# Expert weights of a mixture-of-experts layer: pieces of half the rows by all columns instead of all rows by half the columns

## Chip, cores and metric

One NeuronCore of a Trainium2 chip runs the whole program. The metric is the device time of one execution in microseconds (us). The kernel before took 2630.31 us, the median of three runs (2628.85 to 2637.18).

## The reference, cut to what matters

2048 tokens of width 1024 go through one layer: modulation, grouped attention beside a short convolution, an output projection, and then a mixture of 32 experts (4 groups, top 1; then top 2 of 8 experts). Everything is fp32. The part that the change touches is the norm ahead of the router and the experts:

```python
hx2 = rms_norm(x_new, norm2_g) * (1.0 + sc2) + sh2
...
def expert_block(args):
    xb, e = args
    return (jax.nn.silu(xb @ w_gate[e]) * (xb @ w_up[e])) @ w_down[e]
```

`w_gate` and `w_up` are 1024 x 768 per expert, `w_down` is 768 x 1024. Each expert's output row is scaled by the router's weight, summed over the token's two experts, gated and added to the stream; a last RMSNorm follows.

## The kernel before

**Stages.** Projections, attention and convolution take roughly the first 1440 us. In the stage called out_prep and the functions proj, norm2, logits and route (lines 704 to 950) each of 16 tiles of 128 tokens gets its output projection, the second norm (norm2, lines 816 to 820, result h2 stored to DRAM as h2d) and its routing. From about 1560 us on the 32 experts run, one after the other, in an order (PLAN, line 43) that mixes experts with many and with few tokens. The list CAPS (line 40) holds the padded token count C of each; 20 of them are above 128 (called wide here), 12 are 128 or below (narrow).

**Weights as a stream.** An expert's weights are six pieces of 1.5 MB (piece_src, line 1134). A piece of gate or up is all 1024 rows by 384 of the 768 columns, and a piece of down all 768 rows by 512 of the 1024 columns. Row k*128 + p lands in partition p, so a partition receives 8 runs of 1536 bytes for gate and up, and 6 runs of 2048 bytes for down. The DMA writes fp32 into a ring of five raw tiles (NRAW, line 46), issued by SP in line 1169. Stream.step (line 1173) then takes a third of a raw piece: ACT writes the fp16 high half (line 1192), and DVE subtracts it to make the fp16 low half (line 1194). Three steps finish a piece in a ring of six ready tiles wr. A raw tile is loaded again when its third step is done; a ready tile is written again when its piece is given back (done, line 1209).

**An expert.** Three matmuls (three, lines 1337 to 1340: high by high, high by low, low by high) stand for one fp32 product. gate_up (line 1342) goes over two column halves; for each of three column blocks f of a half it runs 24 matmuls into PSUM tile pg with the gate piece, then 24 into pu with the up piece. ACT makes silu of pg (sg, line 1356), DVE multiplies by pu (line 1357), ACT casts the product to the high half of a (line 1358), DVE makes the low half (line 1359). Three conversion steps follow each f but the last. For a wide expert, down (line 1369) then makes eight blocks of 128 columns in pairs: for both of a pair f = 0 to 4 first, 30 matmuls, and f = 5 behind them. For a narrow expert, down_rows (line 1387) streams 512 columns against the 128 or fewer tokens. Beside the gate and up groups, an iterator (beside, line 1514) transposes the previous expert's outputs and the next expert's gathered rows.

**What sets the order.** The program is written in the order above, and a scheduler places each engine's instructions; each engine then runs its own list strictly in order, so an instruction that waits holds back all behind it. The last two experts' pieces are interleaved in the same raw ring with six loads of acc for the final norm (final_item, line 1451).

Of the kernel before, what the change touches and what calls it, by code (L numbers as in the profile page):

```python
# [9 lines left out]
F32 = mybir.dt.float32  # L10
# [4 lines left out]
AF = mybir.ActivationFunctionType  # L15
OP = mybir.AluOpType
# [3 lines left out]
P = 128  # L20
D = 1024
S = 2048
CTX = 256
KT = D // P
# [8 lines left out]
DE = 768  # L33
FT = DE // P
# [24 lines left out]
def tile_block(ctx: ExitStack, tc: tile.TileContext, x, c, ctxt, c_ctx, w_mod, b_mod, norm1_g, w_in,  # L59
# [370 lines left out]
    if True:  # L430
# [267 lines left out]
        def mod_bc(i):  # L698
            return bass.AP(tensor=modrow.tensor, offset=modrow.offset + i * D, ap=[[0, P], [1, D]])
# [4 lines left out]
        def out_prep():  # L704
# [14 lines left out]
            nc.sync.dma_start(g2, bc(norm2_g, 0, D))  # L719
            B2 = dm["B2"] = dp.tile([P, D], F32, name="B2")  # L720
            nc.sync.dma_start(B2, mod_bc(SH2))

# [7 lines left out]
            yield  # L730
            V.scalar_tensor_tensor(A2, A2, 1.0, g2, op0=OP.add, op1=OP.mult)
            V.scalar_tensor_tensor(mc[:, 1], mc[:, 1], 1.0, mc[:, 2], op0=OP.add, op1=OP.mult)
            yield
# [3 lines left out]
            cB = dm["cB"] = dp.tile([P, NG + NE], F32, name="cB")  # L737
            V.tensor_copy(cB, pl[:, 0:NG + NE])
            yield
            for k in range(KT):  # L740
# [33 lines left out]
        def proj(bp, mf, mh, ml, xt, tt, banks, eng):  # L774
# [355 lines left out]
    wr_pool = [w1] * NEARLY  # L1130
    HE = DE // 2
    PW = KT * HE

    def piece_src(e, i):
        if i < 4:
            src = (w_gate, w_up)[i % 2][0, bass.ds(e, 1)].rearrange("a (k p) n -> p (a k) n", p=P)
            return src[:, :, (i // 2) * HE:(i // 2 + 1) * HE], KT
        src = w_down[0, bass.ds(e, 1)].rearrange("a (k p) n -> p (a k) n", p=P)
        return src[:, :, (i - 4) * 512:(i - 3) * 512], FT

    class Stream:
# [62 lines left out]
        def get(self, q):  # L1204
            while self.piece <= q:
                assert self.step()
            return self.ready[q].rearrange("p a (k n) -> p a k n", k=KT if q % 6 < 4 else FT)

# [91 lines left out]
    with ExitStack() as st:  # L1300
# [16 lines left out]
        def gather(il):  # L1317
            xg = []
            for i, (t, o, n) in enumerate(il):
                g_ = xp.tile([P, D], F32, name=f"xg{i}", bufs=3 - i)  # L1320
                G.indirect_dma_start(out=g_[:n, :], out_offset=None, in_=h2d[:, :],
                                     in_offset=bass.IndirectOffsetOnAxis(ap=t[:n, 0:1], axis=0))
                xg.append(g_)
            return xg

        def transposes(il, xg, xs):
            for (t, o, n), g_ in zip(il, xg):
                for b in range(2):
# [6 lines left out]
                    yield  # L1335

        def three(p_, w, k, cs, x, C, first, last):
            T.matmul(p_[:, :C], w[:, 0, k, cs], x[:, 0, k, :C], start=first, stop=False)  # L1338
            T.matmul(p_[:, :C], w[:, 0, k, cs], x[:, 1, k, :C], start=False, stop=False)  # L1339
            T.matmul(p_[:, :C], w[:, 1, k, cs], x[:, 0, k, :C], start=False, stop=last)  # L1340

        def gate_up(x, ws, q0, C, side=iter(())):
            a = xp.tile([P, 2, FT, CM], F16, name="a")
            for hf in range(2):
                gw, uw = ws.get(q0 + 2 * hf), ws.get(q0 + 2 * hf + 1)
                for f3 in range(3):
                    f = hf * 3 + f3
                    ps = []
                    for w, tag in ((gw, "pg"), (uw, "pu")):
                        p_ = pp.tile([P, 512], F32, name=tag)  # L1350
                        for k in range(KT):
                            three(p_, w, k, slice(f3 * P, (f3 + 1) * P), x, C, k == 0, k == KT - 1)
                        ps.append(p_)
                        next(side, None)
                    sg = sp.tile([P, CM], F32, name="sg")
                    A.activation(sg[:, :C], ps[0][:, :C], AF.Silu, scale=1.0 / WS)  # L1356
                    V.scalar_tensor_tensor(sg[:, :C], ps[1][:, :C], 1.0 / WS, sg[:, :C], op0=OP.mult, op1=OP.mult)  # L1357
                    A.copy(a[:, 0, f, :C], sg[:, :C])
                    V.tensor_sub(a[:, 1, f, :C], sg[:, :C], a[:, 0, f, :C])
                    for _ in range(3 if f < FT - 1 else 0):  # L1360
                        ws.step()
                ws.done(q0 + 2 * hf)
                ws.done(q0 + 2 * hf + 1)
            for w in side:
                if w == "wait":
                    break
            return a

        def down(a, ws, q0, C):
            yT = xp.tile([P, KT, CM], F32, name="yT")  # L1370
            for b in range(2):
                w = ws.get(q0 + 4 + b)
                for d2 in range(0, 4, 2):
                    py = [pp.tile([P, 512], F32, name=tag) for tag in ("pg", "pu")]
                    for fs in (range(FT - 1), (FT - 1,)):
                        for i in range(2):
                            for f in fs:
                                three(py[i], w, f, slice((d2 + i) * P, (d2 + i + 1) * P), a, C, f == 0, f == FT - 1)
                    for i in range(2):
                        d = b * 4 + d2 + i  # L1380
                        A.activation(yT[:, d, :C], py[i][:, :C], AF.Copy, scale=gt2c[:, d:d + 1])
                    ws.step()
                ws.done(q0 + 4 + b)
            return yT


        def down_rows(il, a, ws, q0):
            (t, o, n), = il
            y = sp.tile([P, D], F32, name="y", bufs=3)
            ws_ = [ws.get(q0 + 4 + b) for b in range(2)]  # L1390
            py = [pp.tile([P, 512], F32, name=tag) for tag in ("pg", "pu")]
            for fs in (range(FT - 1), (FT - 1,)):
                for b in range(2):
                    for f in fs:
                        for i, j in ((0, 0), (0, 1), (1, 0)):
                            T.matmul(py[b][:n, :], a[:, i, f, :n], ws_[b][:, j, f, :],
                                     start=(f == 0 and i + j == 0), stop=(f == FT - 1 and i == 1))
            for b in range(2):
                V.scalar_tensor_tensor(y[:n, b * 512:(b + 1) * 512], py[b][:n, :], t[:n, 1:2].bitcast(F32),
                                       gt2r[:n, b * 512:(b + 1) * 512], op0=OP.mult, op1=OP.mult)  # L1400
                ws.step()
                ws.step()
                ws.done(q0 + 4 + b)
            return t, n, y
# [202 lines left out]
```

## Time and profile before

| | us |
|---|---|
| median of 3 runs | 2630.31 |
| lowest and highest run | 2628.85, 2637.18 |
| the profiled execution | 2625.82 |
| its span, first to last instruction | 2624.0 |
| PE busy over the span | 2333.0 |
| DVE busy | 2064.2 |
| ACT busy | 1678.6 |

The profiled execution is 4.5 us below the median, and 1.8 us of it lie outside the span. Matmuls overlap each other in the profile (each is shown with its full latency, while one starts every 50 to 90 ns), so that short gaps of PE are covered by the record of the matmul before; the shares are read by stage, and waits from the list of waits.

### The profile page before, as it was taken

To read this page: it belongs to the slowest core of one execution; us is meant where nothing else is said; L and a number is where in the kernel's file an instruction comes from. 1 tells how busy PE (TensorE), PEld (TensorE's weight loads), DVE (VectorE), ACT (ScalarE), POOL (GpSimd) and SP (SyncE) were. 2 spreads that over 40 slices of the span, in tenths; PEclk is the share of its full clock that TensorE was granted. 3 is DMA by queue.
4 is the path that set the end of the run, shared out by engine and by line. 5 is a ranking of instruction groups with operands and counts; after the bars stand their busy time and mean duration, and the time that the engine had idled before them with its cause. 6 is when DMAs were issued, how large, how long until landed. Compare 5 with 4: busy or idle time off the path is not lost. (4 is left out here: it accounts for less than half of the span.)

```text
span 2624.0 us, 65043 instructions
## 1 busy us (share of the span) xinstructions
PE 2333.0 (89%) x26923; PEld 1791.5 (68%) x26923; DVE 2064.2 (79%) x3558; ACT 1678.6 (64%) x3170; POOL 726.3 (28%) x449
## 2 busy tenths in 40 slices
PE   7878898898999999888889949999999999999974
PEld 2545565665777755555555539998899988999953
DVE  4786789999777788878897657788788887788866
ACT  4554365566666676556656427777677777888854
POOL 2554114322222234435444331111111111211122
PEclk9888999999999999889998969999999999999987
DMA  7422423323111143212211569999999999999996
GB/s 279 145 90 88 127 78 115 125 82 108 50 52 34 34 93 81 64 52 80 58 64 52 191 197 336 338 326 304 307 355 350 349 334 344 340 335 340 358 311 247
DMA packets 320331, 499.27 MB, mean 190 GB/s; under 512 B 50466, under 2 KB 229022, under 8 KB 316959
## 3 DMA queue, kind: packets, MB, share of 16 engines
q1 hardware_dynamic: 281142, 429.41, 48.7%
q0 software_dynamic: 16032, 39.85, 6.0%
q10 hardware_dynamic: 22856, 25.82, 2.9%
q8 instruction: 212, 3.47, 0.5%
q14 instruction: 89, 0.72, 0.1%
HBM read 427.20 MB, written 67.90 MB: 189 GB/s over the span
## 5 line engine op out<-in xcount | busy, mean ns | idle before, releaser
L1194 DVE SCALAR_TENSOR_TENSOR wr<-raw,wr 128x1024 f16<-128x1024 f32 x576 | 685.4, 1218 | 118.8 <-ACT wr L1192 111.3
L1192 ACT ACTIVATE wr<-raw 128x1024 f16<-128x1024 f32 x576 | 580.4, 1054 | 57.3 <-DMA raw<-in_w_up_dram 22.9
L489 ACT ACTIVATE pf<-st 128x512 f32<-128x512 f32 x576 | 345.0, 599 | 284.2 <-PE st L488 226.9
L496 POOL TENSOR_TENSOR pl<-pf,ph 128x1024 f16<-128x1024 f32 x125 | 273.5, 2188 | 620.0 <-PE o L514 259.3
L461 DVE TENSOR_REDUCE mx<-mxp 128x1 f32<-128x512 f32 (+1 forms) x640 | 391.9, 628 | 65.1 <-PE mxp L460 63.6
L1339 PEld LDWEIGHTS <-wr 128*128 128x128 f16 x4032 | 397.4, 99 | 27.6 <-issue 24.6
L1340 PEld LDWEIGHTS <-wr 128*128 128x128 f16 x4032 | 397.2, 99 | 14.4 <-issue 9.9
L1338 PEld LDWEIGHTS <-wr 128*128 128x128 f16 x4032 | 397.1, 99 | 14.1 <-issue 11.3
L490 ACT ACTIVATE ph<-st 128x512 f16<-128x512 f32 x576 | 344.6, 598 | 0.0
L1338 PE MATMUL pg<-x,wr 128*128 128x152 f16 (+19 forms) x1536 | 293.9, 226 | 6.7 <-ACT sg L1356 3.8
L1338 PE MATMUL pu<-x,wr 128*128 128x152 f16 (+19 forms) x1536 | 293.7, 226 | 5.2 <-DVE sg L1357 5.1
L1340 PE MATMUL pu<-x,wr 128*128 128x152 f16 (+19 forms) x1536 | 293.1, 226 | 1.6 <-DVE wr L1194 0.8
L1340 PE MATMUL pg<-x,wr 128*128 128x152 f16 (+19 forms) x1536 | 293.5, 226 | 1.1 <-DVE wr L1194 1.0
L1339 PE MATMUL pg<-x,wr 128*128 128x152 f16 (+19 forms) x1536 | 293.8, 226 | 0.0
L1339 PE MATMUL pu<-x,wr 128*128 128x152 f16 (+19 forms) x1536 | 293.5, 226 | 0.0
L613 PE MATMUL z<-h,cwh 128*128 128x256 f16 x1536 | 275.1, 275 | 12.9 <-DVE vb L621 8.9
L460 PE MATMUL mxp<-k1T,q 128*128 128x512 f16 (+1 forms) x640 | 230.9, 364 | 41.5 <-DVE mx L461 40.5
L514 PE MATMUL o<-vh,pl 128*128 128x65 f16 x2304 | 246.2, 196 | 7.0 <-DVE pl L498 4.6
L512 PE MATMUL o<-vh,ph 128*128 128x65 f16 x2304 | 247.0, 197 | 0.3 <-ACT ob L521 0.2
L513 PE MATMUL o<-vlo,ph 128*128 128x64 f16 x2304 | 246.8, 195 | 0.0
L512 PEld LDWEIGHTS <-ph 128*128 128x128 f16 x2304 | 217.6, 99 | 25.2 <-issue 9.8
L487 PE MATMUL st<-q,k1T 128*128 128x512 f16 x576 | 222.5, 387 | 12.4 <-ACT ph L490 11.9
(349 smaller groups left out, 5541.6 us busy)
## 6 DMA issues: line engine op xcount, KB each, us to landing
raw<-in_w_down_dram SPq DMA_DIRECT2D x64, 1536.0 KB
raw<-in_w_gate_dram SPq DMA_DIRECT2D x63, 1536.0 KB
raw<-in_w_up_dram SPq DMA_DIRECT2D x63, 1536.0 KB
xt<-in_x_dram SPq DMA_DIRECT2D x32, 512.0 KB
h<-hs SPq DMA_DIRECT2D x16, 1024.0 KB
wmod<-in_w_mod_dram SPq DMA_DIRECT2D x64, 256.0 KB
w<-in_w_mod_dram SPq DMA_DIRECT2D x16, 512.0 KB
hs<-h ACTq DMA_DIRECT2D x8, 1024.0 KB
```

Source lines behind the costliest of these rows:

```text
L461: V.tensor_reduce(rowmax[u][:, j, i:i + 1], p_[:, :n], axis=AX.X, op=OP.max)
L489: A.activation(pf[:, i], p_, AF.Exp)
L490: A.activation(ph[:, i], p_, AF.Exp)
L496: G.tensor_tensor(pl, pf, ph, op=OP.subtract)
L512: T.matmul(po[:, j], ph[:, i, js], vh1[:, k, g], start=f, stop=False, skip_group_check=True)
L513: T.matmul(po[:, j, 0:HD], ph[:, i, js], vlo[:, k, g], start=False, stop=False, skip_group_check=True)
L613: T.matmul(z, w_[:, k, cs], h[:, a_, k, :], start=(n == 0), stop=(n == 3 * KT - 1))
L1192: A.activation(w[:, 0, sl], t[:, sl], AF.Copy, scale=WS)
L1194: V.scalar_tensor_tensor(w[:, 1, sl], t[:, sl], WS, w[:, 0, sl], op0=OP.mult, op1=OP.subtract)
L1338: T.matmul(p_[:, :C], w[:, 0, k, cs], x[:, 0, k, :C], start=first, stop=False)
L1339: T.matmul(p_[:, :C], w[:, 0, k, cs], x[:, 1, k, :C], start=False, stop=False)
L1340: T.matmul(p_[:, :C], w[:, 1, k, cs], x[:, 0, k, :C], start=False, stop=last)
```

## The change

A piece is now half the rows by all columns. The six pieces of an expert are gate, gate, up, up, down, down. For gate and up the rows are dealt so that partition p holds rows 8p to 8p+7; four of them by 768 columns lie one behind the other in DRAM, one run of 12288 bytes for each partition. A piece of down is three runs of 3072 bytes for each partition. The piece sizes, the rings, the conversions and the matmuls are the same in number and in shape.

Because row 8p + k now belongs to contraction step k, the normed tokens have to be dealt likewise: norm2 writes column 8q + k of the norm to place 128k + q (the multiply reads x and A2 with a step of 8 elements), and the shift B2 is copied once into the dealt order.

With a product needing both pieces of a matrix, gate_up runs its six gate groups first and its six up groups behind them. The silu of all six blocks is kept in one sg tile. One conversion step follows every group, and six follow in down, where both pieces are held to the end. The gathered rows have two buffers for each of their two tiles instead of three and two.

```diff
-    HE = DE // 2
-    PW = KT * HE
+    KN = (KT // 2, KT // 2, FT // 2)
+    PW = KT // 2 * DE
 
     def piece_src(e, i):
+        kn = KN[i // 2]
+        w_ = (w_gate, w_up, w_down)[i // 2][0, bass.ds(e, 1)]
         if i < 4:
-            src = (w_gate, w_up)[i % 2][0, bass.ds(e, 1)].rearrange("a (k p) n -> p (a k) n", p=P)
-            return src[:, :, (i // 2) * HE:(i // 2 + 1) * HE], KT
-        src = w_down[0, bass.ds(e, 1)].rearrange("a (k p) n -> p (a k) n", p=P)
-        return src[:, :, (i - 4) * 512:(i - 3) * 512], FT
+            src = w_.rearrange("a (p k) n -> p (a k) n", p=P)
+        else:
+            src = w_.rearrange("a (k p) n -> p (a k) n", p=P)
+        return src[:, (i % 2) * kn:(i % 2 + 1) * kn, :], kn
...
+        def dealt(t):
+            return t.rearrange("p (q k) -> p k q", k=KT)
+
         def norm2(bp, xt, r, eng):
             h2 = bp.tile([P, D], F32, name="h2")
-            V.scalar_tensor_tensor(h2, xt, r, dm["A2"], op0=OP.mult, op1=OP.mult)
+            V.scalar_tensor_tensor(h2.rearrange("p (k q) -> p k q", k=KT), dealt(xt), r, dealt(dm["A2"]), op0=OP.mult, op1=OP.mult)
...
+            B2 = dm["B2"] = dp.tile([P, D], F32, name="B2")
+            V.tensor_copy(B2.rearrange("p (k q) -> p k q", k=KT), dealt(b2))
...
-                g_ = xp.tile([P, D], F32, name=f"xg{i}", bufs=3 - i)
+                g_ = xp.tile([P, D], F32, name=f"xg{i}", bufs=2)
...
         def gate_up(x, ws, q0, C, side=iter(())):
             a = xp.tile([P, 2, FT, CM], F16, name="a")
-            for hf in range(2):
-                gw, uw = ws.get(q0 + 2 * hf), ws.get(q0 + 2 * hf + 1)
-                for f3 in range(3):
-                    f = hf * 3 + f3
...
+            sg = sp.tile([P, FT, CM], F32, name="sg", bufs=1)
+            for m in range(2):
+                w = ws.both(q0 + 2 * m)
+                for f in range(FT):
+                    p_ = pp.tile([P, 512], F32, name=("pg", "pu")[f % 2])
+                    for k in range(KT):
+                        three(p_, w, k, slice(f * P, (f + 1) * P), x, C, k == 0, k == KT - 1)
+                    next(side, None)
+                    if m == 0:
+                        A.activation(sg[:, f, :C], p_[:, :C], AF.Silu, scale=1.0 / WS)
+                    else:
+                        V.scalar_tensor_tensor(sg[:, f, :C], p_[:, :C], 1.0 / WS, sg[:, f, :C], op0=OP.mult, op1=OP.mult)
+                        A.copy(a[:, 0, f, :C], sg[:, f, :C])
+                        V.tensor_sub(a[:, 1, f, :C], sg[:, f, :C], a[:, 0, f, :C])
+                    ws.step()
+                ws.done(q0 + 2 * m)
+                ws.done(q0 + 2 * m + 1)
...
         def down(a, ws, q0, C):
             yT = xp.tile([P, KT, CM], F32, name="yT")
-            for b in range(2):
-                w = ws.get(q0 + 4 + b)
-                for d2 in range(0, 4, 2):
...
+            w = ws.both(q0 + 4)
+            for d in range(0, KT, 2):
...
+                for _ in range(1 + d // 2 % 2):
                     ws.step()
-                ws.done(q0 + 4 + b)
+            ws.done(q0 + 4)
+            ws.done(q0 + 5)
             return yT
```

The loads on SP's queue, around one expert of the middle of the stage (raw is a raw tile; the numbers behind the names are partitions by elements), before:

```order
L1169 DMA raw<-in_w_down_dram 128x6x512
L1169 ISA
L1169 DMA raw<-in_w_down_dram 128x6x512
L1169 ISA
L1169 DMA raw<-in_w_gate_dram 128x8x384
L1169 ISA
L1169 DMA raw<-in_w_up_dram 128x8x384
```

and with the change:

```order
L1178 DMA raw<-in_w_down_dram 128x3x1024
L1178 ISA
L1178 DMA raw<-in_w_gate_dram 128x3072
L1178 ISA
L1178 DMA raw<-in_w_gate_dram 128x3072
L1178 ISA
L1178 DMA raw<-in_w_up_dram 128x3072
```

The number of loads and their place among the others stay; a load of gate or up is one run of 3072 elements for each partition instead of eight of 384.

ACT at the end of gate_up of the wide expert with C = 148, where down begins (a is the product's high half, yT the output of down), before:

```order
L1356 ACTIVATE sg<-pg 128x148
L1358 CAST a<-sg 128x148
L1356 ACTIVATE sg<-pg 128x148
L1192 ACTIVATE wr<-raw 128x1024 x3
L1358 CAST a<-sg 128x148
L1192 ACTIVATE wr<-raw 128x1024 x2
L1381 ACTIVATE yT<-pg,gt2c 128x148
```

and with the change:

```order
L1201 ACTIVATE wr<-raw 128x1024
L1371 CAST a<-sg 128x148 x4
L1201 ACTIVATE wr<-raw 128x1024 x2
L1371 CAST a<-sg 128x148
L1201 ACTIVATE wr<-raw 128x1024 x2
L1391 ACTIVATE yT<-pg,gt2c 128x148
```

The cast of the last block, f = 5, stood behind three conversions and now stands behind two, and the four casts before it stand together.

DVE in the up groups of the same expert, with the change (sg is the product, wr the low half of a conversion):

```order
L1370 SCALAR_TENSOR_TENSOR sg<-pu,sg 128x148
L1203 SCALAR_TENSOR_TENSOR wr<-raw,wr 128x1024
L1372 TENSOR_TENSOR a<-sg,a 128x148
L1370 SCALAR_TENSOR_TENSOR sg<-pg,sg 128x148
L1372 TENSOR_TENSOR a<-sg,a 128x148
L1370 SCALAR_TENSOR_TENSOR sg<-pu,sg 128x148
L1203 SCALAR_TENSOR_TENSOR wr<-raw,wr 128x1024
L1372 TENSOR_TENSOR a<-sg,a 128x148
L1203 SCALAR_TENSOR_TENSOR wr<-raw,wr 128x1024 x11
```

The multiplications and subtractions of all six blocks stand in one phase with five conversions between them, and eleven conversions in a row follow.

## Rows read from the trace of the kernel before

**Rows 1.** The page: span, mean busy share of the DMA engines, GB/s, 40 slices.

```profile
span 2624.0 us, 65043 instructions
...
DMA  7422423323111143212211569999999999999996
GB/s 279 145 90 88 127 78 115 125 82 108 50 52 34 34 93 81 64 52 80 58 64 52 191 197 336 338 326 304 307 355 350 349 334 344 340 335 340 358 311 247
```

**Rows 2.** Windows: us, then busy PE, PEld, DVE, ACT, POOL; clock, DMA share, GB/s.

```profile
1600.00:1790.00 190.00, 189.22 (x2434) 178.02 (x2432) 151.19 (x200) 144.59 (x240) 35.13 (x19) 1.00 1.02 329
1790.00:2200.00 410.00, 387.21 (x5138) 361.50 (x5137) 335.14 (x445) 302.62 (x502) 64.16 (x40) 0.99 1.01 336
2200.00:2490.00 290.00, 281.30 (x4300) 274.27 (x4298) 233.26 (x312) 238.89 (x428) 48.07 (x34) 0.99 1.03 344
2490.00:2624.00 134.00, 77.78 (x980) 60.29 (x977) 86.44 (x126) 68.06 (x120) 30.99 (x31) 0.82 0.79 281
```

**Rows 3.** Waits from 1790 to 2200 us: total, times, longest.

```profile
ACT wr L1192 <- DMA raw<-in_w_up_dram: 19.5, 10, 4.8
ACT wr L1192 <- DMA raw<-in_w_down_dram: 16.5, 12, 4.1
...
PE pg L1338 <- ACT a L1358: 13.0, 8, 3.5
...
ACT wr L1192 <- DMA raw<-in_w_gate_dram: 6.7, 3, 3.4
...
PE pg L1339 <- DVE a L1359: 3.6, 7, 0.5
```

**Rows 4.** Waits from 2200 to 2490 us.

```profile
PE pg L1338 <- ACT a L1358: 5.7, 9, 1.1
...
PE pg L1339 <- DVE a L1359: 2.1, 8, 0.5
...
ACT wr L1192 <- DMA raw<-in_w_up_dram: 0.9, 1, 0.9
```

**Rows 5.** Timeline of ACT at 2195 us: start, duration, idle before and its releaser.

```profile
2195.36 2.95 ACT L1192 ACTIVATE wr<-raw 128x1024 f16<-128x1024 f32 x3 [3.39 <-DMA raw<-in_w_gate_dram]
```

**Rows 6.** Timeline of PE around the same place.

```profile
2193.78 0.23 PE L1339 MATMUL pg<-a,wr 128*128 128x152 f16 x1
...
2194.84 0.23 PE L1340 MATMUL pu<-a,wr 128*128 128x152 f16 x1
2198.57 0.23 PE L1338 MATMUL pg<-a,wr 128*128 128x152 f16 x1 [3.51 <-ACT a L1358]
```

**Rows 7.** DMA queues from 1700 to 2200 us: packets, MB, share of 16 engines.

```profile
q1 hardware_dynamic: 91076, 146.10, 84.8%
q0 software_dynamic: 8544, 19.21, 16.0%
```

**Rows 8.** DMA queue from 30 to 39 us, x, w_mod and w_in loads.

```profile
q1 hardware_dynamic: 1085, 3.67, 102.0%
```

**Rows 9.** DMA issues from 2490 to 2600 us: expert weights.

```profile
raw<-in_w_down_dram SPq DMA_DIRECT2D x4, 1536.0 KB
raw<-in_w_up_dram SPq DMA_DIRECT2D x3, 1536.0 KB
raw<-in_w_gate_dram SPq DMA_DIRECT2D x2, 1536.0 KB
```

**Rows 10.** Instructions from 2200 to 2490 us: count, busy us, mean ns.

```profile
L1192 ACT ACTIVATE wr<-raw 128x1024 f16<-128x1024 f32 x169 | 171.5, 1056 | 0.9 <-DMA raw<-in_w_up_dram 0.9
...
L1358 ACT CAST a<-sg 128x148 f16<-128x148 f32 x6 | 1.9, 310 | 6.3 <-DVE sg L1357 6.3
...
L1194 DVE SCALAR_TENSOR_TENSOR wr<-raw,wr 128x1024 f16<-128x1024 f32 x170 | 201.4, 1219 | 28.6 <-ACT wr L1192 24.3 <-issue 3.2
...
L1357 DVE SCALAR_TENSOR_TENSOR sg<-pu,sg 128x148 f32<-128x148 f32 x6 | 1.8, 304 | 2.5 <-PE ty L1412 2.5
```

**Rows 11.** Line 818: ns min/median/max.

```profile
L818 DVE SCALAR_TENSOR_TENSOR h<-xt,n2r,A x16: 1264/1285/3155, 1012.7 to 1529.8; 128x1024 f32<-128x1024 f32 x16
```

More of the change, by code (lines that the diff above doesn't have):

```diff
@@ L731, in out_prep @@
             V.scalar_tensor_tensor(A2, A2, 1.0, g2, op0=OP.add, op1=OP.mult)
+            b2 = dp.tile([P, D], F32, name="h2")
+            nc.sync.dma_start(b2, mod_bc(SH2))
             V.scalar_tensor_tensor(mc[:, 1], mc[:, 1], 1.0, mc[:, 2], op0=OP.add, op1=OP.mult)
@@ L1206, in get, with both @@
                 assert self.step()
-            return self.ready[q].rearrange("p a (k n) -> p a k n", k=KT if q % 6 < 4 else FT)
+            return self.ready[q].rearrange("p a (k n) -> p a k n", k=KN[q % 6 // 2])
+        def both(self, q):
+            return self.get(q), self.get(q + 1)
         def done(self, q):
@@ L1337, in three @@
         def three(p_, w, k, cs, x, C, first, last):
-            T.matmul(p_[:, :C], w[:, 0, k, cs], x[:, 0, k, :C], start=first, stop=False)
-            T.matmul(p_[:, :C], w[:, 0, k, cs], x[:, 1, k, :C], start=False, stop=False)
-            T.matmul(p_[:, :C], w[:, 1, k, cs], x[:, 0, k, :C], start=False, stop=last)
+            n = w[0].shape[2]
+            w_, kk = w[k // n], k % n
+            T.matmul(p_[:, :C], w_[:, 0, kk, cs], x[:, 0, k, :C], start=first, stop=False)
+            T.matmul(p_[:, :C], w_[:, 0, kk, cs], x[:, 1, k, :C], start=False, stop=False)
@@ L1342, in gate_up @@
+            T.matmul(p_[:, :C], w_[:, 1, kk, cs], x[:, 0, k, :C], start=False, stop=last)
         def gate_up(x, ws, q0, C, side=iter(())):
             a = xp.tile([P, 2, FT, CM], F16, name="a")
-            for hf in range(2):
-                gw, uw = ws.get(q0 + 2 * hf), ws.get(q0 + 2 * hf + 1)
-                for f3 in range(3):
-                    f = hf * 3 + f3
[L1348 to L1363, printed above, removed]
@@ L1370, in down @@
             yT = xp.tile([P, KT, CM], F32, name="yT")
-            for b in range(2):
-                w = ws.get(q0 + 4 + b)
-                for d2 in range(0, 4, 2):
[L1374 to L1378, printed above, removed]
-                    for i in range(2):
-                        d = b * 4 + d2 + i
-                        A.activation(yT[:, d, :C], py[i][:, :C], AF.Copy, scale=gt2c[:, d:d + 1])
+            w = ws.both(q0 + 4)
+            for d in range(0, KT, 2):
+                py = [pp.tile([P, 512], F32, name=tag) for tag in ("pg", "pu")]
+                for fs in (range(FT - 1), (FT - 1,)):
+                    for i in range(2):
+                        for f in fs:
+                            three(py[i], w, f, slice((d + i) * P, (d + i + 1) * P), a, C, f == 0, f == FT - 1)
+                for i in range(2):
+                    A.activation(yT[:, d + i, :C], py[i][:, :C], AF.Copy, scale=gt2c[:, d + i:d + i + 1])
+                for _ in range(1 + d // 2 % 2):
                     ws.step()
-                ws.done(q0 + 4 + b)
+            ws.done(q0 + 4)
+            ws.done(q0 + 5)
             return yT
@@ L1389, in down_rows @@
             y = sp.tile([P, D], F32, name="y", bufs=3)
-            ws_ = [ws.get(q0 + 4 + b) for b in range(2)]
+            w = ws.both(q0 + 4)
             py = [pp.tile([P, 512], F32, name=tag) for tag in ("pg", "pu")]
@@ L1395, in down_rows @@
                         for i, j in ((0, 0), (0, 1), (1, 0)):
-                            T.matmul(py[b][:n, :], a[:, i, f, :n], ws_[b][:, j, f, :],
+                            T.matmul(py[b][:n, :], a[:, i, f, :n], w[f // 3][:, j, f % 3, b * 512:(b + 1) * 512],
                                      start=(f == 0 and i + j == 0), stop=(f == FT - 1 and i == 1))
@@ L1400, in down_rows @@
                                        gt2r[:n, b * 512:(b + 1) * 512], op0=OP.mult, op1=OP.mult)
-                ws.step()
-                ws.step()
+                for _ in range(3):
+                    ws.step()
                 ws.done(q0 + 4 + b)
```

3 lines of the change are left out of this document (1 added, 2 removed).

## The prediction, made before the changed kernel ran

> **What bounds the kernel now.** I read the page's slices first. From slice 24 on (about 1575 us) the sixteen DMA engines are busy nine tenths or more almost to the end, at 300 to 358 GB/s [rows 1]. That is the expert stage, the last 1050 us, and only there does the change alter much. Cut into four windows [rows 2], the stage shows two engines at their limit together: from 1600 to 2490 us the DMA share is 1.01 to 1.03, and PE is busy 189.2 of 190, 387.2 of 410 and 281.3 of 290 us. PE stands still for 22.8 us from 1790 to 2200 and for 8.7 us from 2200 to 2490. In the last 134 us PE works only 77.8 us.
>
> Who makes PE wait tells the windows apart. From 1790 to 2200 ACT waits 42.7 us (19.5 + 16.5 + 6.7), 25 times, for raw weights that have not landed, and PE waits 13.0 us, 8 times, for ACT's cast of a [rows 3]. One such place in full: at 2195.36 ACT starts three conversions after 3.39 us of idle for a gate piece [rows 5]; the cast of f = 5 stands behind them, and PE, which had started a matmul every 66 ns (17 from 2193.78 to 2194.84), stands still for 3.51 us [rows 6]. From 2200 to 2490 ACT waits 0.9 us for weights, and PE's 9 waits for the cast come to 5.7 us [rows 4]: 0.6 us each instead of 1.6. So in the first stretch late weights set the pace, in the second PE does, with a short wait at the start of down that comes from conversions ahead of the cast.
>
> **The change, part by part.** The profiled execution took 2625.8 us, 4.5 below the median of 2630.3; I work the sum out against the former and add the 4.5 back.
>
> *Longer runs.* From 1700 to 2200 us the weights' queue moved 146.10 MB in 84.8% of 500 us [rows 7], 344.6 GB/s while busy; its packets have 1604 bytes on average (146.10 MB / 91076). From 30 to 39 us the same queue moved 3.67 MB in 102% of 9 us, 400 GB/s, with packets of 3382 bytes [rows 8]. The change makes gate and up packets 12288 bytes (or whatever pieces the engines cut these into) and those of down 3072. No row has 12288, and the bounds are 345 (nothing gained) and something above 400. I take 400, since both new sizes are nearer to the second row. The 146.10 MB then need 365 us instead of 424. With the 16.0% of the gathers and scatters [rows 7] the engines would be busy 0.73 + 0.16 = 0.89 of the stretch: the transfer stops being the limit there, with a tenth to spare.
>
> The Trainium skill, "DMA: Bandwidth & Descriptors", section Specifications, gives 512 bytes as the minimum transfer for line rate. By that rule the 1536 bytes of before are at full rate already and this term is nothing. The two queue rows disagree with it, 345 against 400 GB/s, though they lie in different stages.
>
> *Late weights, 1790 to 2200.* Of PE's 22.8 us, a residue like that of the next window stays: 8.7 us over 9 waits there, so 7.7 us for 8. That removes 15 us. Bounds: 0, if weights land as late as now, and 22.8. From 1600 to 1790 PE lost 0.8 us, so nothing is to be had there.
>
> *The wait at the start of down.* The residue in both windows is 7.7 + 8.7 = 16.4 us. In the new order ACT's last cast stands behind two conversions instead of three, one of 1.056 us less [rows 10]. Against waits of 0.6 us that could remove all of it; but DVE now does all six multiplications and subtractions of an expert in one phase. In six groups of 24 matmuls, 6 x 24 x 66 ns = 9.5 us of PE, DVE has six multiplications of 0.304, six subtractions that I take as equally long, and five conversions of 1.219 us [rows 10], 9.7 us. ACT has six casts of 0.310 and five conversions, 7.1 us. DVE just keeps up, and the 30 matmuls that down does ahead of f = 5 cover 30 x 66 ns = 2.0 us of lag. I take half, 8 us. Bounds: 0 and 16.
>
> *The end.* Nine weight pieces of 1.573 MB are issued from 2490 to 2600 [rows 9], 14.2 MB: 41.1 us at 344.6 GB/s, 35.4 at 400. That is 5.7 us less for a queue on which the last two experts wait; but loads of acc and stores of the output share the raw ring there, so I take 4. Bounds: 0 and 8.
>
> *Costs.* The multiply of norm2, 16 times 1.285 us on DVE [rows 11], now reads two operands with a step of 32 bytes. No row of this kernel has such a read. Between 0 and a doubling, 20.6 us of DVE, all but the last tile stands beside attention and projection work of PE. I take 2 us, for the last tile and for the shift of one turn in the order of that stage. The copy of B2, of the same size as the multiply, is once 1.3 us on DVE, beside attention. The order of the gate groups costs nothing: silu of all blocks takes the same six instructions. The gathers lose a buffer, but each is issued an expert ahead of its transposes, and an expert takes 1050 / 32 = 33 us. Both pieces of down are now held to the end of down; their next conversions stand in the following gate groups, an up phase before they are needed, so this is hidden as long as weights are not later than about 9.5 us. A gather's 4 KB rows will take turns with packets of up to 12 KB; that is hidden by the same lead.
>
> Sum: 15 + 8 + 4 - 2 = 25 us. 2625.8 - 25 = 2600.8, and 4.5 more for the median: **2605 us**.
>
> **The rivals.** About 0.3%, 8 us, is what a measurement of this kernel can tell from no change.
>
> *More than that.* If PE runs without waits from 1790 to 2490 (22.8 + 8.7) and the end gives 8: 2630.3 - 39.5 + 2 = 2593. For it: DMA would have a tenth to spare. Against: the tight DVE sum above.
>
> *The runs were not what limits the weights.* Either 1536 bytes were long enough (the rule above), or the memory gives no more while gathers and scatters run beside. Then the first and the third term vanish, and 8 - 2 = 6 us are left: 2624. For it: no stretch with long packets and scatters together exists in the trace. Against: the two rates.
>
> *Strided reads of the norm.* If the multiply takes twice its 1.285 us and DVE, busy most of that stage, delays all of it, 20.6 - 2 more than I count: 2605 + 18.6 = 2624. The Trainium skill, "SBUF — State Buffer", section "Door 1: The DMA port swizzle", says that accesses that go to a new 16-byte line each time pay a penalty; a step of 32 bytes does. No run here shows the size. Against: 15 of the 16 have other work beside them.
>
> *Slower: the up phase closes into a loop.* Multiply, cast, ACT's conversion, DVE's conversion, next multiply: 0.304 + 0.310 + 1.056 + 1.219 = 2.9 us per group against PE's 24 x 66 ns = 1.6. The order breaks this loop by putting the next multiply behind the subtraction and four casts together. If it closes in four of six groups, because some conversion waits for weights in between, DVE is 4 x 1.3 = 5.2 us late at the end of gate_up, 3.2 more than the 2.0 that down covers. Over the 20 wide experts that is 64 us in place of the 16.4 of now: 2630.3 - (15 + 4 - 2) + (64 - 16.4) = 2661. It outweighs the 17 us gained from 2.1 us of wait per wide expert on, 4.1 us of lag. For it: DVE's sum has no room. Against: the order as it stands.
>
> **How the numbers follow.** Forecast 0.68, more 0.09, the runs 0.09, strided reads 0.05, loop 0.09. Faster by over 0.3% (below 2622.4) are forecast and more: 0.77. Within are the runs and the strided reads: 0.14. Slower is the loop: 0.09. The range runs from 2584 (all upper bounds, 22.8 + 16 + 8, without cost: 2583.5) to 2630; it takes in the two cases of no change and leaves out the loop and some of the edges.
>
> **What would show it.** Right: between 1700 and 2200 us the weights' queue has some tens of thousands fewer packets and a rate near 400 GB/s while busy; ACT's 42.7 us of waits for raw fall below 10; PE's waits for the cast keep to 0.6 us or less each; the DMA share in the middle falls below 1. Wrong: the queue's rate stays near 345; or PE waits for sg or a by more than 2 us at the start of down; or the norm's multiply takes 2 us and more and the first matmul of the experts comes later.

## The result, and the profile after

The change made the kernel slower: 2649.46 us (median of 8 runs, 2643.45 to 2664.0) against 2631.84 for the kernel before (8 runs beside them), a ratio of 1.0070, 95% interval 1.0050 to 1.0091. I had forecast 2605, with 0.09 for slower, and the time lies outside the range of 2584 to 2630. The profiled execution took 2648.57 us, span 2646.8, against 2625.82 and 2624.0 before.

First the page: the span, and the DMA engines over 40 slices of 66 us.

```profile
span 2646.8 us, 64879 instructions
...
DMA  7432424333111142211212358999999999999985
GB/s 281 141 97 76 126 79 123 114 94 97 52 49 34 36 101 67 70 51 61 59 53 64 141 179 297 351 319 325 343 334 366 358 345 347 345 349 349 335 319 215
```

Against [rows 1], slices 22 to 24 (from 1456 us) have fallen from 191, 197, 336 to 141, 179, 297 GB/s. The expert weights start later, so the loss begins ahead of the stage that the change was about. Where it stands is read from two instructions. The first expert matmul, in the kernel before and with the change (line: count, ns min/median/max, first and last start):

```profile
L1338 PE MATMUL pg<-x,wr x1536: 206/224/334, 1565.5 to 2578.6; 128*128 128x152 f16 x24, 128*128 128x120 f16 x18, 128*128 128x140 f16 x18, 128*128 128x136 f16 x18
```

```profile
L1353 PE MATMUL pg<-x,wr x1536: 206/224/334, 1598.1 to 2596.3; 128*128 128x152 f16 x24, 128*128 128x120 f16 x18, 128*128 128x140 f16 x18, 128*128 128x136 f16 x18
```

And the first matmul of the last expert but two (timelines of PE, before and with the change), behind which the end stage begins:

```profile
2489.01 0.21 PE L1338 MATMUL pg<-x,wr 128*128 128x112 f16 x1
```

```profile
2503.16 0.21 PE L1353 MATMUL pg<-x,wr 128*128 128x112 f16 x1
```

This cuts the execution in three:

| us | before | after | difference |
|---|---|---|---|
| up to the first expert matmul | 1565.5 | 1598.1 | +32.6 |
| from there to the last expert but two | 923.5 | 905.1 | -18.4 |
| from there to the end of the span | 135.0 | 143.6 | +8.6 |
| span | 2624.0 | 2646.8 | +22.8 |

The middle part came near its forecast of 23 us (15 + 8). Windows (columns as in [rows 2]), the waits from 1790 to 2200 us, and the DMA queues from 1700 to 2200:

```profile
1600.00:1790.00 190.00, 186.25 (x2379) 175.60 (x2380) 144.42 (x195) 136.94 (x227) 33.22 (x16) 0.98 0.94 332
1790.00:2200.00 410.00, 398.91 (x5331) 372.10 (x5330) 342.21 (x453) 318.40 (x528) 73.04 (x40) 1.00 0.97 345
2200.00:2490.00 290.00, 284.90 (x4360) 278.00 (x4358) 238.47 (x321) 240.33 (x428) 53.66 (x37) 1.00 0.98 348
2490.00:2646.00 156.00, 94.21 (x1189) 74.20 (x1186) 101.07 (x147) 81.30 (x142) 31.49 (x32) 0.80 0.75 276
```

```profile
ACT wr L1201 <- DMA raw<-in_w_down_dram: 12.9, 9, 4.8
...
PE tq L1344 <- DMA xg<-h2d,il: 5.4, 2, 3.0
...
PE pg L1353 <- ACT sg L1368: 1.6, 1, 1.6
PE pg L1353 <- ACT a L1371: 1.0, 3, 0.5
```

```profile
q1 hardware_dynamic: 24654, 150.63, 79.2%
q0 software_dynamic: 8224, 19.35, 16.3%
```

PE's idle time from 1790 to 2200 has fallen from 22.8 to 11.1 us. ACT's 42.7 us of waits for raw weights [rows 3] are 12.9, all for down pieces, and PE's waits for the cast of a (the fp16 high half of the product) are 1.0 us in place of 13.0. The queue moves 150.63 MB / (0.792 x 500 us) = 380 GB/s while busy, 344.6 before [rows 7]. New is PE's wait of 5.4 us for gathered tokens.

Ahead of the experts one row has changed most, the multiply of norm2 ([rows 11] before):

```profile
L825 DVE SCALAR_TENSOR_TENSOR h<-xt,n2r,A x16: 2053/2095/6006, 1013.6 to 1561.8; 128x1024 f32<-128x1024 f32 x16
```

It takes 2.095 us in place of 1.285, and the last of the 16 starts 32.0 us later. 16 times 0.81 is 13.0 us, so this row alone cannot make the 32.6.

### The profile page after: what moved, and what is told of

Read it like the earlier page. It is cut to its first block, busy times and chain, and to the rows that moved or that the text cites. A ratio compares the mean times of both kernels' runs of the same rounds, so it can differ in the third digit from the quotient of the medians.

```text
span 2646.8 us, 64879 instructions
## 1 busy us (share of the span) xinstructions
PE 2345.7 (89%) x26923; PEld 1794.8 (68%) x26923; DVE 2076.8 (78%) x3559; ACT 1681.0 (64%) x3170; POOL 745.2 (28%) x449
## 5 line engine op out<-in xcount | busy, mean ns | idle before, releaser
L1201 ACT ACTIVATE wr<-raw 128x1024 f16<-128x1024 f32 x576 | 586.3, 1054 | 67.2 <-issue 20.7
```

The costliest lines, as they stand in the source:

```text
L1201: A.activation(w[:, 0, sl], t[:, sl], AF.Copy, scale=WS)
```

## The experiments

All ratios are to the kernel before, run beside each kernel; the differences below are differences of these ratios times 2631 us.

**Plain norm2, long runs kept.** norm2 and the load of B2 are those of the kernel before; the transposes of the gathered tokens do the deal.

```diff
-V.scalar_tensor_tensor(h2.rearrange("p (k q) -> p k q", k=KT), dealt(xt), r, dealt(dm["A2"]), ...)
+V.scalar_tensor_tensor(h2, xt, r, dm["A2"], ...)
-            V.tensor_copy(B2.rearrange("p (k q) -> p k q", k=KT), dealt(b2))
-            yield
...
-T.transpose(tq[:, k, :n], g_[:n, (b * 4 + k) * P:(b * 4 + k + 1) * P], ident[:n, :n])
+T.transpose(tq[:, k, :n], dealt(g_)[:n, b * 4 + k, :], ident[:n, :n])
```

> The changed kernel with norm2 and the shift B2 as they were before (natural order, no copy, no added step); the transposes of the gathered tokens read every eighth column instead, so the long runs of the weights stay. Three theories for the 32.6 us by which the first expert matmul starts later (1565.5 us before, 1598.1 us now). S, the strided multiply: 2.10 us in place of 1.285 us, 16 times, on a VectorE whose results the attention stage waits for; then the start comes back to 1565 to 1572 us. O, the added step of the preparation and the later load of B2: the same here, since both are gone. D, the long packets of the first weights delay the small list scatters (median 4.4 us to landing, 2.9 before): the start stays late by the one step seen at the last tiles, about 7 us, at 1572 us. In each case the stage from the first expert to the last but two stays near 905 us (before 923.5): S and O together predict 2620 us, D 2627 us. If the strided read costs TensorE something in the transposes, the expert stage is longer than 905 us.

Measured 2624.23 us, ratio 0.9978 (0.9962 to 0.9995). The first expert matmul is at 1573.1 us, the stretch behind it 907.8:

```profile
L1350 PE MATMUL pg<-x,wr x1536: 206/224/334, 1573.1 to 2572.6; 128*128 128x152 f16 x24, 128*128 128x120 f16 x18, 128*128 128x140 f16 x18, 128*128 128x136 f16 x18
```

So norm2, B2 and their step are what made the change slower. Between S and D this run does not decide, since 1573 is nearer to D's number, and 3.6 us of its lateness against the kernel before is there at 946 us already (last start of the matmuls of line 613: 946.2 against 942.6), ahead of the first norm2. Drifts of a few us show in other traces too.

**The deal alone, on the kernel before.** Weights `(p k)`, in pieces of half the columns by all rows; norm2 and B2 as in the change.

> The kernel before with the dealt norm2 and B2 of the change (strided multiply, copy, added step), and gate and up rows p*8+k, but in pieces of half the columns by all rows as before, so the weights keep runs of 1536 bytes. S and O: the first expert matmul is as late as in the changed kernel but for the list step, 1588 to 1592 us, and the time is 25 us above before, 2655 to 2660 us. D: the long packets are gone and the start is back near 1565 us if they alone did it; list scatters land in 2.9 us again and VectorE does not wait 7 us for them. A plain bystander (none of the three): 2632 us.

2663.44 us, ratio 1.0113 (1.0091 to 1.0134), first expert matmul at 1601.0, later than the 1588 to 1592 that S and O gave it. Without a single long packet the stage ahead of the experts is as late as with the change, and VectorE still waits 6.7 us for the scatters (9.7 with the change, 4.8 before). D falls as the cause of the late start.

**The change without the added step.**

```diff
             V.tensor_copy(B2.rearrange("p (k q) -> p k q", k=KT), dealt(b2))
-            yield
```

> The changed kernel without the added step: the copy that deals B2 stands in the same step as the scaling of the router's weights. The strided multiply stays. O: the attention stage goes back to the order of before, the first expert matmul starts by 15 to 25 us earlier than 1598 us, total 2625 to 2635 us. S: no change, 2649 us within 3 us. D: no change.

2636.61 us, ratio 1.0019 (1.0005 to 1.0033), first expert matmul at 1586.3. O holds in kind and falls short in size: the time is about 13 us less than with the change, and the start 11.8 us earlier in place of 15 to 25. The rest of the delay stays, and so does the strided multiply.

**Two buffers for the routing entries.**

```diff
-            en = sp.tile([P, 2, 2, 2], I32, name="en")
+            en = sp.tile([P, 2, 2, 2], I32, name="en", bufs=2)
```

> The changed kernel with two buffers for the routing entries en, so that the next pair of tiles does not wait until the scatters of the last pair have read theirs. D: the 7 us that VectorE waited for the scatters (9.7 us in two waits; 4.8 us before) go, and the start of the experts comes 6 to 9 us earlier, total 2641 to 2644 us. S and O: at most the 4.8 us that were there before, 2645 to 2649 us.

2653.74 us, ratio 1.0076 (1.0049 to 1.0102), and VectorE still waits 7.9 us: the scheduler moved the copy into en up by a pair of tiles, ahead of the same scatters. D's wait was not removed, so this run says nothing for or against it.

**No deal at all.** The first kernel of this section with both rearrangements taken back:

```diff
         if i < 4:
-            src = w_.rearrange("a (p k) n -> p (a k) n", p=P)
+            src = w_.rearrange("a (k p) n -> p (a k) n", p=P)
...
-T.transpose(tq[:, k, :n], dealt(g_)[:n, b * 4 + k, :], ident[:n, :n])
+T.transpose(tq[:, k, :n], g_[:n, (b * 4 + k) * P:(b * 4 + k + 1) * P], ident[:n, :n])
```

> The changed kernel's pieces (half the rows by all columns) without any deal: row k*128+p on partition p, so a gate or up run is one row, 3072 bytes; norm2, B2 and the transposes are those of the kernel before. If the gain of the expert stage comes from the length of the runs (from 1536 to 12288 bytes) in proportion, 3072 bytes give about half of it: the stretch from the first expert to the last but two, 923.5 us before and 905.1 with the change, comes to 912 to 915 us. If it comes from a run of a whole row at 3072 bytes or more, or from the pieces themselves (gate before up, both down pieces at hand), it comes to 905 us. If the 12 KB are needed, it stays at 918 to 923 us. The attention stage is that of before: first expert at 1565 to 1573 us. Total by these: 2625, 2617, or 2632 us. Small transfers: the gathers of tokens take 9.0 us from issue to landing beside 1536-byte packets, 17 us beside 12288; if the packet length does it, 10 to 12 us here.

2614.69 us, ratio 0.9937 (0.9924 to 0.9950), the fastest kernel of the study and faster than both. First expert matmul at 1570.4, the stretch behind it 902.5. Runs of 3072 bytes give all that the 12 KB gave. PE's waits for gathered tokens in that stretch are gone. How far a stretch of one trace can be trusted is seen where the expert code is the same: it is 902.0 to 910.6 us in six kernels with 3072-byte runs, and 905.1 to 909.2 in the four with 12 KB and plain transposes (the change among them). Stretches that differ by less than some 8 us decide nothing by themselves. The queues of the kernel without a deal from 1700 to 2200 us:

```profile
q1 hardware_dynamic: 49524, 151.97, 82.4%
q0 software_dynamic: 8544, 19.21, 16.1%
```

369 GB/s while busy: less than the 380 of the 12 KB runs, and the stage is no longer for it.

**The late rows' reduction ahead of their scatter**, with no deal, and with the 12 KB runs and plain norm2. In the end stage with the change, PE stands still for 9.1 us, up to 2563.15, and POOL's timeline (start, duration, idle before and its releaser) shows a gather ahead of the small power `fr` that DVE waits for:

```profile
2547.56 2.00 POOL L1453 DMA_INDIRECT acc<-xg,il  x1 [0.20 <-issue]
2549.58 0.73 POOL L117 TENSOR_TENSOR nfr<-nfv,mhalf 128x1 f32<-128x1 f32 x1
2558.55 1.06 POOL L1446 DMA_INDIRECT xg<-acc,il  x1 [8.24 <-DMA acc<-xg,il]
2559.64 0.58 POOL L1440 TENSOR_TENSOR fr<-fvar,mhalf 112x1 f32<-112x1 f32 x1
```

```diff
+            norm_rows(y, g_, n)
             if last:
-                norm_rows(y, g_, n)
                 late_out(t, n, y)
             G.indirect_dma_start(out=acc[:, :], out_offset=at_rows(t, n), in_=g_[:n, :], in_offset=None)
             if not last:
                 yield
-                norm_rows(y, g_, n)
```

> The same, and in the late rows the reduction of the normed row is written ahead of the scatter to acc, which puts the small power on POOL ahead of the next gather, as in the kernel before (in the changed kernel it stands behind a gather that waits 8.2 us for the scatter, and TensorE idles for 9.3 us in gate and up of the last expert but one). If that order is what costs in the end stage, the last 143.6 us come to 134 to 138 us, 5 to 8 us less than the same kernel without it. If the end is set by the weights of the last two experts, it moves by less than 2 us.

> Plain norm2 with the 12 KB runs (columns dealt in the transposes), and the order of the late rows mended as in the two others. Against the same kernel without it (2624.2 us) 5 to 8 us less if that order costs in the end stage, 2617 to 2619 us; within 2 us if the weights set the end.

2616.61 us (0.9945, 0.9931 to 0.9959) and 2628.43 (0.9982, 0.9967 to 0.9998), each within the interval of the same kernel without it. On POOL the power did move ahead, to 2520.51 us with the gather at 2526.07 (without a deal; 2526.23 behind a gather at 2525.15 without the edit), but PE's longest wait in that gate and up only fell from 7.4 to 5.5 us, and from 8.7 to 7.4 in the other kernel. The theory that this order makes the end longer falls; what the gap waits for next was not followed further.

**The place of the final items** (`FIN`, where the loads of acc for the last norm stand among the last weights; first on the kernel without a deal and with the late rows' edit, then without that edit):

```diff
-FIN, AHEAD = (3, 5, 7, 13, 14, 15), 4
+FIN, AHEAD = (3, 5, 7, 13, 14, 17), 4
```

> The same as the one before, and the sixth final item (one tile) comes behind both down pieces of the last expert instead of ahead of them. TensorE waits 13 to 18 us for these two pieces before its last matmuls; one tile of 512 KB and its multiply less ahead of them is worth 1 to 3 us, if the load and not the order of the last rows decides; nothing if the rows of the last expert wait for the final items anyway.

2620.59 us, ratio 0.9963 (0.9950 to 0.9977): slower by 0.0018 than without it, though the intervals overlap. The other way, `(3, 5, 7, 12, 13, 14)`:

> The kernel without a deal, with the last three final items one place earlier, ahead of the second up piece of the last expert in place of behind it. TensorE waits 18.7 us in the last expert's second half for its down pieces and 10 us in its gate and up; a later place of one item cost 4 us (2620.6 against 2616.6). If the items' place decides, 2 to 4 us less; if the sum of the loads does, the same within 2 us.

2619.32 us, ratio 0.9942 (0.9926 to 0.9958), the same as without it (0.9937).

**Long runs alone.**

```diff
         if i < 4:
-            src = w_.rearrange("a (k p) n -> p (a k) n", p=P)
+            src = w_.rearrange("a (p k) n -> p (a k) n", p=P)
```

> The kernel without a deal (2614.7 us), but with gate and up rows in contiguous runs of 12 KB while the tokens' columns stay in natural order: rows and columns are paired wrongly, all sizes and the order of the work are the same. It tells what the step from 3072 to 12288 bytes does by itself. If longer runs go on helping, 5 to 10 us less, 2605 to 2610. If 3 KB are as good and the long packets only delay the gathers beside them (TensorE waited 5.4 us for gathered tokens in the expert stage with the change, not at all with 3072-byte runs), 0 to 8 us more, 2615 to 2623; then the 9.5 us between the versions with 12 KB by strided transposes (2624.2) and with none are shared between these and the strided transposes.

2622.36 us, ratio 0.9957 (0.9940 to 0.9974): the step from 3072 to 12288 bytes costs 0.0020, 5 us, though its interval overlaps that of the kernel without a deal, so that a cost of nothing is not ruled out. The stretch of the experts is 908.4 us, within the spread of the kernels with 3072 bytes. What does tell the two apart are waits for gathered tokens (waits of PE, 1575 to 2490 us):

```profile
PE tq L1341 <- DMA xg<-h2d,il: 9.5, 3, 6.9
```

From 1605 to 2470 us PE waits for them 4.5 to 11.2 us in five of the six kernels with 12 KB, and 0.7 us at most in the six with 3072 bytes.

From here to the kernel with strided transposes (0.9978) are another 0.0021, 5.5 us, but the intervals overlap and the stretches are 908.4 and 907.8 us: that the strided transposes cost time is not shown. That each of their weight loads takes longer is (grouped by shape from 1800 to 2470 us, first strided, then plain in the kernel without a deal; 145 ns in the kernel with long runs alone):

```profile
L1341 PEld LDWEIGHTS tq<-ident,xg 128*128 128x128 f32 x120 | 15.9, 196 | 4.6 <-DMA xg<-h2d,il 4.6
```

```profile
L1341 PEld LDWEIGHTS tq<-ident,xg 128*128 128x128 f32 x120 | 12.7, 141 | 0.0
```

**The strided multiply alone, and the step alone**, each put on the kernel without a deal:

```diff
-            V.scalar_tensor_tensor(h2, xt, r, dm["A2"], op0=OP.mult, op1=OP.mult)
+            V.scalar_tensor_tensor(h2.rearrange("p (k q) -> p k q", k=KT), dealt(xt), r, dealt(dm["A2"]), op0=OP.mult, op1=OP.mult)
```

> The kernel without a deal, with the strided multiply of norm2 alone put back (16 times 2.1 in place of 1.285 us); B2, its load and the steps stay as before, so the shift is added to columns in another order than theirs and the experts' result is wrong. S: the first expert matmul comes 8 to 16 us later (1570.4 us without it), total 2623 to 2631 us. If the strided multiply is hidden and the late load or the copy of B2 cost it, within 3 us of 2614.7.

```diff
             V.tensor_copy(cB, pl[:, 0:NG + NE])
             yield
+            yield
             for k in range(KT):
```

> The kernel without a deal, with an empty step in the preparation at the place of the added one: no instruction more, only the pieces of the output stage dealt to the attention stage one place later. O: the first expert matmul comes 8 to 16 us later than 1570.4 us, total 2623 to 2631 us. If the copy and load of B2 in that step cost it, within 3 us of 2614.7.

2633.5 us, ratio 0.9984 (0.9969 to 0.9998), and 2635.73, ratio 1.0004 (0.9993 to 1.0015). The multiply costs 0.0047, 12 us, and the empty step 0.0067, 18 us, each within about 5 us. In the trace of the multiply the first expert matmul is at 1590.6, in that of the step at 1589.8, both some 20 us behind 1570.4. The two work differently. The windows from 1100 to 1300 us, in the middle of attention, without a deal and then with the step alone, the latter with two pairs of 10 us from the same stretch:

```profile
1100.00:1300.00 200.00, 171.15 (x1813) 104.60 (x1810) 167.22 (x321) 116.79 (x238) 94.45 (x55) 0.94 0.22 66
```

```profile
1100.00:1300.00 200.00, 169.69 (x1647) 103.38 (x1646) 157.28 (x282) 106.73 (x215) 81.03 (x49) 0.87 0.18 58
1150.00:1160.00 10.00, 6.46 (x70) 3.56 (x69) 9.46 (x13) 4.02 (x8) 4.92 (x3) 0.90 0.30 104
1160.00:1170.00 10.00, 9.29 (x52) 6.23 (x51) 4.88 (x17) 2.02 (x5) 0.00 (x0) 0.50 0.34 81
1200.00:1210.00 10.00, 5.33 (x48) 2.94 (x46) 6.60 (x8) 3.93 (x8) 7.57 (x6) 0.96 0.14 53
1210.00:1220.00 10.00, 8.46 (x77) 5.68 (x77) 6.23 (x13) 3.84 (x7) 1.77 (x1) 0.70 0.44 128
```

PE is busy as long as before, 169.7 against 171.2 us, but starts 1647 matmuls and not 1813, which is near the ratio of the granted clocks, 0.87 and 0.94 (1813 x 0.87 / 0.94 = 1678). By that, 0.07 of 200 us, 14 us at full clock, is an estimate of what the clock takes in this stretch. In the two pairs it falls behind 10 us in which PE was busy 6.5 and 5.3: to 0.50, which is 1.2 GHz throughout, and to 0.70. Two pairs make no rule: without a deal PE is busy 5.9 us from 1200 to 1210, at 0.83, and the next 10 us are at 1.00. The window with the multiply alone keeps 0.94:

```profile
1100.00:1300.00 200.00, 166.35 (x1736) 99.42 (x1735) 168.46 (x310) 114.71 (x234) 91.88 (x53) 0.94 0.21 64
```

There PE is busy 4.8 us less and DVE 1.2 more: PE waits for a VectorE that has more to do, for its row maxima (mx) and the router's logits (L). PE's waits from 1100 to 1300 us, without a deal and with the multiply:

```profile
PE mxp L460 <- DVE mx L461: 17.4, 10, 4.4
...
PE ms L468 <- DVE L L843: 2.5, 1, 2.5
```

```profile
PE mxp L460 <- DVE mx L461: 19.3, 9, 4.4
PE ms L468 <- DVE L L843: 5.3, 1, 5.3
```

Over this stretch the clock is 0.86 or 0.87 in all four kernels with the added step (the change, the one with two en buffers, the deal alone, the step alone), 0.91 in the change without that step, and 0.92 to 0.95 in the kernel before and the ten others without it.

**Short runs again, on the new pieces.** Only gate and up go back to 1536 bytes; runs of down stay at 4096.

```diff
-                        self.queue.dma_start(t.rearrange("p (k n) -> p k n", k=k), src)
+                        td, c = t.rearrange("p (k n) -> p k n", k=k), src.shape[2] // (2 if i < 4 else 1)
+                        for c0 in range(0, src.shape[2], c):
+                            self.queue.dma_start(td[:, :, c0:c0 + c], src[:, :, c0:c0 + c])
```

> The kernel without a deal (2614.7 us, 0.9937 of before), its gate and up pieces loaded in two transfers of half the columns each, so that their runs are 1536 bytes again while the pieces, the order of the work and the computation stay. If the run length gives the expert stage its gain (first expert to last but two: 923.5 us before, 902.5 without a deal), it goes back to 915 to 925 us and the time to 2627 to 2636 us. If the shape of the pieces gives it (gate ahead of up, both down pieces at hand), it stays at 902 to 907 us, total 2614 to 2620.

2628.03 us, ratio 0.9979 (0.9967 to 0.9990), the stretch of the experts 912.4 us: between the two expectations. In the time the step to 3072 bytes is clear of the intervals, 0.0042 or 11 us. Of the 21.0 us from 923.5 to 902.5 the run length of gate and up gives 9.9 by these single traces, and the shape and order of the pieces 11.1, in which down's runs grow from 2048 to 4096 bytes as well. The queue moves 148.45 MB in 84.7% of 500 us, 351 GB/s. ACT's waits for raw (1790 to 2200 us) are back, and PE's waits for the cast are not:

```profile
ACT wr L1200 <- DMA raw<-in_w_down_dram: 28.3, 12, 7.1
...
ACT wr L1200 <- DMA raw<-in_w_up_dram: 5.4, 2, 4.2
```

```profile
PE pg L1352 <- ACT a L1370: 1.9, 5, 0.5
```

With 0.8 us for gate ACT waits 34.5 us for weights here, 42.7 before; PE idles 16.6 us, 4.8 of them for gathered tokens, against 22.8. So late weights alone do not stop PE: for other reasons than tokens it stands 11.8 us where it stood 22.8, with ACT's waits four fifths of what they were.

The gathers take 16.2 us to land beside these packets (8.9 before, 17.4 with the change, median from issue, 1600 to 2490 us), so the length of the packets is not what doubles that time.

**One gather buffer less, on the kernel before.**

```diff
-                g_ = xp.tile([P, D], F32, name=f"xg{i}", bufs=3 - i)
+                g_ = xp.tile([P, D], F32, name=f"xg{i}", bufs=2)
```

> The kernel before with two buffers for each tile of gathered rows, as in the change (one less for the first), and nothing else. The gathers take 9.0 us from issue to landing (median) before, 9.6 with the deal alone, and 15 to 22 us in every kernel with the new pieces, whether their packets are 1536, 3072 or 12288 bytes long. If the lost buffer does it, 15 us or more here, and TensorE waits some us for gathered rows; if the new order of the pieces does it, 9 to 10 us here. The time: 2631 us within 4 us if the lead of an expert covers it, as I assumed; 2635 to 2645 if not.

2629.35 us, ratio 0.9998 (0.9983 to 1.0013), gathers 8.6 us: on the kernel before it is not the buffer either. It comes with the new pieces; by what, stays open.

## Why the prediction was wrong, point by point

**The costs are the step that failed.** "I take 2 us, for the last tile and for the shift of one turn in the order of that stage" was 32.6 us in the trace, 30 by the two runs that took it apart. That is 28 of the 44 us by which 2605 missed. Most of the rest are gains that did not come: 27 us forecast, 12 by the first three rows of the table below. The prediction's own sign for a late start, a multiply of 2 us and more and a later first matmul, is what the trace showed.

- "All but the last tile stands beside attention and projection work of PE" took PE's work as a cover for DVE's. The multiply grew by 0.81 us, near the middle of my bounds, but 12 us, give or take 5, reached the end, out of 13.0. DVE is busy 167 of 200 us in that stage without a deal, and its results (the row maxima above all) are what PE waits for. My rival "strided reads of the norm" had this mechanism at 0.05; it should have been a term of the sum. The Trainium skill, "SBUF — State Buffer", section "Door 1: The DMA port swizzle", names a penalty for accesses that reach a new 16-byte line each time; the trace agrees, with 2.095 us at a step of 32 bytes against 1.285.
- "The shift of one turn in the order" I priced by the instructions that it adds, none. The step alone, empty, costs 18 us. It moves every later piece of the output stage against the attention work; shown is that the granted clock from 1100 to 1300 us then is 0.87 in place of 0.94, by the estimate above 14 us of the 18. Which of the moved pieces opens these gaps is not settled.

| part | from | to | difference, us |
|---|---|---|---|
| shape and order of the pieces, down's runs with them | 1.0000 | 0.9979 | -6 |
| gate and up runs of 1536 to 3072 bytes | 0.9979 | 0.9937 | -11 |
| gate and up runs of 3072 to 12288 | 0.9937 | 0.9957 | +5 |
| strided multiply | 0.9937 | 0.9984 | +12 |
| added step | 0.9937 | 1.0004 | +18 |

The five differences sum to 0.0071, and the change measured 0.0070. The deal alone gives 1 + 0.0047 + 0.0067 = 1.0114 by the same rows and measured 1.0113. Each row carries an interval of about 0.002 to either side, so the fit is closer than it had to be: by the same rows the change without the step would be 1.0004, and it measured 1.0019.

**Longer runs: the rate right, the gain not.** 400 GB/s forecast, 380 measured; the DMA share from 1790 to 2200 fell from 1.01 to 0.97 only, where 0.89 was forecast, and ACT's waits for raw to 12.9 us, not below 10. Beside the rule of the Trainium skill, "DMA: Bandwidth & Descriptors", section Specifications (512 bytes suffice for line rate), the rows stand against it from 1536 to 3072 bytes, 351 to 369 GB/s and 11 us. Beyond 3072 the rate rises and the time does not fall; there I had no row, and the gain I ascribed to 12 KB is had with 3072, at none of the costs.

**Late weights: the number near, the mechanism in part another.** 15 us forecast; PE idles 11.7 us less from 1790 to 2200. I had put all of it down to weights that arrive sooner, yet with gate and up at 1536 bytes and ACT still waiting 34.5 us PE's waits for the cast are already down from 13.0 to 1.9 us. The new pieces took these away, which I had priced, and by half, in the next term only. **The wait at the start of down:** 8 forecast. PE's 13.0 us of waits for the cast there are 1.0, and from 2200 to 2490 PE idles 5.1 us in place of 8.7. Together 23 forecast, 18.4 measured over the whole stretch; gathers that land late take back some of it (5.4 us of PE's waits). That wait I had called hidden by the lead of an expert.

**The end: wrong sign.** 4 us of gain forecast, 8.6 of loss in the trace. PE's idle time grew in the last experts, the DMA engines moved 276 GB/s from 2490 us on (281 before, [rows 2]) in a longer time, and four attempts at its order gained nothing. The end stage is 139.7 to 143.6 us in the six kernels with 12 KB, 137.5 to 139.4 in the four with 3072 bytes and the same final items, 135.0 to 140.0 in the four with 1536. It is longest with the longest runs; what makes it so stays open.

**The slower rival was the wrong one.** The loop of the up phase, 0.09, did not close: PE's waits for a and sg from 1790 to 2200 come to 3.0 us, none longer than 1.6.

**Two errors that changed no term:** a row of down has 1024 columns, so its runs are 4096 bytes and not the 3072 given above. And the loop would outweigh the 17 us from (16.4 + 17) / 20 = 1.7 us of wait per wide expert on, not from 2.1.

## What to carry to other kernels

Price a moved or added turn in an interleaved stage by what the engines wait for there, not by its instructions: an empty one cost 18 us here, more than the 11 us that the best step in run length gained. Before a layout is dealt to lengthen DMA runs, ask for the shortest run that is enough: a whole row of 3072 bytes, which any split by rows gives without a deal, was as good as 12 KB, and the kernel with it, 2614.69 us (0.9937), beats both. An operation is covered only by an engine that does not wait for its engine's queue.

## What the runs showed of the hardware that I had not expected

- TensorE's granted clock over 200 us of attention went from 0.94 to 0.87 by the place of instructions alone, in every kernel with the added step (0.86 or 0.87), at nearly the same busy time where the step stands alone (169.7 and 171.2 us).
- The weights' queue moved 351, 369 and 380 GB/s while busy with gate and up runs of 1536, 3072 and 12288 bytes (down 4096 in all three); the last step brought no time.
- The time from issue to landing of the token gathers went from 8.9 us to 16.2 with the new pieces, gate and up runs of 1536 bytes as before; it was 8.6 with the buffer taken away alone.
- A stationary load of TensorE from fp32 read with a step of 32 bytes took 196 ns against 141, and a VectorE multiply with two such operands 2.095 us against 1.285.
